# One process for both directions of a state recurrence, and a later low part of the weights

## The chip, the cores and the metric

The kernel runs on one core of a Trainium2 chip. The metric is device time in microseconds of one launch, the median over several executions. The engines are TensorE (PE in the profile; PEld is its weight load), VectorE (DVE), ScalarE (ACT), GpSimd (POOL) and SyncE (SP, here a queue for DMAs). Each works through its own queue in program order.

## The reference

It is one layer of a bidirectional encoder, applied with one set of weights to a prompt (512 tokens) and a sample (1024 tokens), width 1024, all in fp32:

```
x = x + 0.5 * gate1 * rmsnorm(swiglu_1(mod(rmsnorm(x))))
z = mod(rmsnorm(x)) @ w_in
x = x + gate2 * rmsnorm([pool_mixer(z_pool) | rwkv7(z_rwkv)] @ w_out)
x = x + 0.5 * gate3 * rmsnorm(swiglu_2(mod(rmsnorm(x))))
```

What the change touches is the recurrence inside `rwkv7`: 8 heads of 64, forward and reversed, each with a 64 x 64 state S:

```
def step(S, inp):
    r_t, w_t, k_t, v_t, na_t, b_t = inp
    sa = einsum('bhvk,bhk->bhv', S, na_t)
    S = S * w_t + sa[..., None] * b_t + v_t[..., None] * k_t
    y = einsum('bhvk,bhk->bhv', S, r_t)
```

## The kernel before, in words

**Dense work.** The tokens stand in three blocks of 512 (two of the sample, one of the prompt), features on the partitions. Every fp32 product with a big weight matrix is made of three matmuls in a reduced fp32 format: high part of the weight by high part of the data, high by low, low by high (`mm3`, line 740). `WStream` (line 483) brings the weights in tiles of 128 x 512 in the order in which they are used: a DMA on SP's queue into one of 5 raw buffers (`wraw`), a copy on ScalarE that rounds to the high part (`whi`, 5 buffers), and a subtraction for the low part (`wlo`, 5 buffers), on GpSimd or VectorE, and during the scan always on VectorE. `get` (line 510) hands out tile i and first writes into the program the high and low parts up to tile i + 3 and the loads up to tile i + 8.

**The scan.** The recurrence is done in chunks of L = 64 tokens. Four chunks make a group (256 tokens); a macro is two groups (`gi` 0 and 1) of one pair of heads, for both directions `d`. There are 12 macros, so 24 groups and 96 chunk steps, each for two directions. For each group `scan_prep` (line 1159) makes the decays and the products between the chunk's keys (ending in a masked copy to `MU`, flag `ba`). `scan_inv` (line 1284) inverts the triangular matrices, in 31 dependent steps on VectorE for gi = 0 and on GpSimd for gi = 1; only one of the two holds the lock `inv` at a time. Then `scan_state` (line 1332) goes through the chunks in three stages:

- W: `SBD` (the state of the two heads as a block diagonal) times `AR`, plus a product of `MA` with the values in `UV`, into a PSUM bank of the direction, partitions 0 to 63, and from there by ScalarE to `iw` (a part of `XN`). In the profile these are `sb<-SBD,AR` and `sb<-MU` (64*64), then ACT `XN<-sb`. Then ScalarE makes `s0p`, the state times its decay.
- U: `MA` times that, also into partitions 0 to 63 (`sb<-XN,MU`), and by ScalarE to the upper half of `UV` (ACT `MU<-sb`).
- Last stage: the update of the state (`sb<-MU,BKt`) and the output (`sb<-AR,SBD` and `sb<-MU` with 128*64), head 0 into partitions 0 to 63 and head 1 into 64 to 127; then VectorE adds to `s0p` and writes the state (`SBD<-sb,PL,s0p`).

In the first chunk of a pair of heads the state is zero, and the products with it are left out. After the last state step of a group `scan_prep` may go on to the same group of the next macro, and at the end of a pair of heads `scan_post` (line 1399) normalizes the output and stores it (`m<-yT`).

**What sets the order.** The kernel writes all instructions in one program order, worked out when it is built. The dense work and each part of the scan are processes (Python generators) with a priority. `Estimate` (line 42) keeps an estimated clock for each engine, and `run_until` (line 217) goes on with the ready process of the highest priority. A process that yields WAIT is ready again 200 ns (state steps) or 400 ns (others) after the estimated end of all that it has just issued. Before the change the two directions are two processes of `scan_state` (line 1585), each with its own readiness; dense work yields after each matmul and fills what is left. Dense work meets the scan twice: `wout_gen(0)` (line 1486) needs the sample's output of the scan, and the output projections of the other blocks need the scan's end (`wouts`, line 1532).

Of the kernel before, what the change touches and what calls it, by code (L numbers as in the profile page):

```python
# [10 lines left out]
F32R = mybir.dt.float32r  # L11
I32 = mybir.dt.int32
AF = mybir.ActivationFunctionType
ALU = mybir.AluOpType
# [3 lines left out]
P = 128  # L18
# [4 lines left out]
TB = 512  # L23
L = 64
# [14 lines left out]
GO, WAIT, CHAIN, PIPE = -1.0, -2.0, -3.0, -4.0  # L39
# [125 lines left out]
def rev(ap):  # L165
    a = [list(x) for x in ap.ap]
    st, n = a[-1]
    a[-1] = [-st, n]
    return bass.AP(tensor=ap.tensor, offset=ap.offset + st * (n - 1), ap=a)
# [3 lines left out]
def encoder_kernel(ctx, tc, x_prompt, x_sample, c_prompt, c_sample, ada_w, ada_b, n1_pre, n1_post,  # L173
# [5 lines left out]
    V, S, G, T, SY = (Queue(est, *q) for q in (("V", nc.vector), ("S", nc.scalar), ("G", nc.gpsimd), ("T", nc.tensor),  # L179
                                               ("Y", nc.sync)))  # L180
# [3 lines left out]
    def nm(s):  # L184
        uid[0] += 1
        return f"{s}{uid[0]}"
# [15 lines left out]
    def mt(shape, tag, bufs, dt=F32, pool=None):  # L202
        return est.ring((pool or mp).tile(shape, dt, name=nm(tag), tag=tag, bufs=bufs), (id(pool), tag), bufs)
# [4 lines left out]
    class Proc:  # L208
        def __init__(self, gen, prio):
            self.gen, self.prio, self.ready, self.cond = gen, prio, est.free["T"], None  # L210
# [3 lines left out]
    def spawn(gen, prio):  # L214
        procs.append(Proc(gen, prio))
# [38 lines left out]
    flags = set()  # L254
    scanning = []
# [22 lines left out]
    def has(*k):  # L278
        return lambda: all(x in flags for x in k)

    def mm(out, lhsT, rhs, start=True, stop=True):
        T.matmul(out, lhsT, rhs, start=start, stop=stop, skip_group_check=True)
# [200 lines left out]
    class WStream:  # L483
        def __init__(self, items):
            self.items, self.raw, self.out = items, {}, {}
            self.i, self.nl, self.ns = 0, 0, 0

        def load(self, upto):
            while self.nl <= min(upto, len(self.items) - 1):
# [6 lines left out]
        def split(self, upto):  # L496
            while self.ns <= min(upto, len(self.items) - 1):
                self.load(self.ns)
                t = self.raw.pop(self.ns)
                wh = mt([P, TB], "whi", 5, F32R)  # L500
                wl = mt([P, TB], "wlo", 5, F32R)
                S.activation(wh, t, AF.Copy)
                now = est.free["T"]
                g_, v_ = max(now, est.free["G"]) + 1200, max(now, est.free["V"]) + 600
                E = G if not scanning and (g_ < now + POOL_LATE or g_ < v_) else V
                E.tensor_tensor(wl, t, wh.bitcast(F32), ALU.subtract)
                self.out[self.ns] = (wh, wl)
                self.ns += 1

        def get(self):  # L510
            i = self.i
            self.i += 1
            self.split(i + 3)
            self.load(i + 8)
            return self.out.pop(i)

    def cols(w, c0):
# [434 lines left out]
    GT = (TB, 2 * TB)  # L952
# [192 lines left out]
    GL = 4 * L  # L1145

    def st_(sb, shape, tag, bufs=1):
        return mt(shape, tag, bufs, pool=sb.sp)
# [180 lines left out]
            flags.add(("inv", m, gi))  # L1329
            give("inv")  # L1330

    def scan_state(sb, d):
        AR, BKt, UV, MA, MR, SBD, PL, bank = sb.AR, sb.BKt, sb.UV, sb.MA, sb.MR, sb.SBD, sb.PL, sb.bank[d]
        Wp = bank[0:64, 0:P]
        Up = bank[0:64, P:2 * P]
        for m, (i_, hf) in enumerate(macros):
            g, p = pairs[i_]
            nblk = GT[g] // GL
            nh = nblk // 2
            for c8 in range(8):  # L1340
                gi, c = c8 // 4, c8 % 4
                if c == 0:
                    yield has(("inv", m, gi))
                zero = hf == 0 and c8 == 0
                lastc = hf == nh - 1 and c8 == 7
                us = [gi * 16 + d * 8 + h * 4 + c for h in range(2)]
                if not zero:
                    mm(Wp, AR[:, gi, d, c, 0, :], SBD[:, d, :], stop=False)
                for h in range(2):
                    mm(Wp[:, h * L:(h + 1) * L], MA[64:128, us[h], :], UV[64:128, gi, d, c, h, :], start=zero)  # L1350
                wsb = sb.iw[:, d * P:(d + 1) * P]
                S.activation(wsb, Wp, AF.Copy)
                if not zero and not lastc:
                    s0p = st_(sb, [P, P], f"s0p{d}")
                    S.activation(s0p, SBD[:, d, :], AF.Copy, scale=PL[:, m % 2, gi, d, c:c + 1])
                yield WAIT
                for h in range(2):
                    mm(Up[:, h * L:(h + 1) * L], MA[0:64, us[h], :], wsb[:, h * L:(h + 1) * L])
                S.activation(UV[0:64, gi, d, c].rearrange("p h f -> p (h f)"), Up, AF.Copy)
                yield WAIT  # L1360
                if not lastc:
                    for h in range(2):
                        hs_ = slice(64 * h, 64 * h + 64)
                        mm(bank[hs_, 0:L], BKt[:, gi, d, c, hs_], UV[:, gi, d, c, h, :])
                yo = 256 + c * L
                if not zero:
                    for h in range(2):
                        hs_ = slice(64 * h, 64 * h + 64)
                        mm(bank[hs_, yo:yo + L], SBD[hs_, d, hs_], AR[hs_, gi, d, c, 1, :], stop=False)
                for h in range(2):  # L1370
                    mm(bank[64 * h:64 * h + 64, yo:yo + L], UV[:, gi, d, c, h, :], MR[:, us[h], :], start=zero)
                if not lastc:
                    for h in range(2):
                        hs_ = slice(64 * h, 64 * h + 64)
                        pl_ = PL[hs_, m % 2, gi, d, c:c + 1]
                        if zero:
                            V.tensor_scalar(SBD[hs_, d, hs_], bank[hs_, 0:L], pl_, None, op0=ALU.mult)
                        else:
                            V.scalar_tensor_tensor(SBD[hs_, d, hs_], bank[hs_, 0:L], pl_, s0p[hs_, hs_],
                                                   ALU.mult, ALU.add)  # L1380
                if c == 3:
                    t = 2 * hf + gi
                    gb = t if d == 0 else nblk - 1 - t
                    if t == 0 and i_ not in sb.yT:
                        if i_ >= 1:
                            yield has(("post", i_ - 1))
                        if i_ not in sb.yT:
                            sb.yT[i_] = st_(sb, [P, GT[g]], "yT")
                    o = sb.yT[i_][:, gb * GL:(gb + 1) * GL]
                    if d == 1:  # L1390
                        o = rev(o)
                    if t >= nh:
                        V.tensor_tensor(o, o, bank[:, 256:512], ALU.add)
                    else:
                        S.activation(o, bank[:, 256:512], AF.Copy)
                    flags.add(("st", m, gi, d))
                yield WAIT

    def scan_post(sb):
# [181 lines left out]
    with tc.tile_pool(name="late", bufs=1, reuse_waits="tile") as lp:  # L1581
        sb = ScanBufs(lp)
        scanning.append(sb)

        spawn(scan_state(sb, 0), 0)
        spawn(scan_state(sb, 1), 0)
        spawn(scan_inv(sb, 0), PRIO_INV)
        spawn(scan_inv(sb, 1), PRIO_INV)
        spawn(scan_prep(sb), PRIO_PREP)
        spawn(scan_post(sb), PRIO_POST)  # L1590

        run_until(has(("m", 1), ("m", 0)))
        scanning.clear()
# [35 lines left out]
```

## Time and profile before

| | us |
|---|---|
| three runs | 3784.39, 3785.25, 3792.80 |
| median | 3785.25 |
| the profiled execution | 3780.28 |
| its span, first to last instruction | 3778.3 |
| TensorE busy | 3593.2 (95%) |
| VectorE busy | 1999.0 (53%) |
| ScalarE busy | 1424.1 (38%) |
| GpSimd busy | 1410.4 (37%) |

The mean granted clock of TensorE is 0.956. The first state step is at 1270.6 us of the span and the last at 2697.4 us. In a row of a group, `out<-in` names tiles, `xN` counts instructions, and behind the bars stand the busy time and the idle time in front of them with what ended it. All instructions are recorded at one helper's line (161), so tiles tell them apart. An fp32 matmul leaves two records. The window rows give busy time per engine in a stretch and the granted clock; the timeline rows give start, duration, engine, instruction; the rows of waits give who waited for whom, the total in us, how often, and the longest.

### The profile page before, as it was taken

The page shows a single profiled execution, that of the slowest core. Times are in us where ns is not written, and L with a number is a line of the kernel's source. Part 1 is how long each engine was busy: PE and PEld are TensorE (multiplying, and loading weights), DVE is VectorE, ACT ScalarE, POOL GpSimd, SP SyncE. Part 2 cuts the span into 40 slices and gives each one's busy share as a digit, 9 for nine tenths or more (in the row PEclk, how much of TensorE's full clock was granted, in tenths as well). Part 3 has the DMA queues.
Part 4 walks back from the last instruction along what each step waited for, and adds up shares of the span by engine and source line. Part 5 has one row for each costly group of instructions (what it writes and reads, how often), then busy time and mean ns, then how long its engine had stood idle before and what let it go on. Part 6 is the DMA issues. An engine that isn't in the chain of part 4 may idle for free. (4 is left out here: it accounts for less than half of the span.)

```text
span 3778.3 us, 53665 instructions
## 1 busy us (share of the span) xinstructions
PE 3593.2 (95%) x19579; PEld 2703.6 (72%) x19579; DVE 1999.0 (53%) x3801; ACT 1424.1 (38%) x2776; POOL 1410.4 (37%) x1716
## 2 busy tenths in 40 slices
PE   7999999998999999999899989799999999999998
PEld 4667878876676767666666666567787778877886
DVE  3128362237237778776777776778448622242223
ACT  3324342225335434344345433343334432234222
POOL 2333444443132222234234233432344344444444
PEclk8999999998999999999889978599999999999999
DMA  7655343334344322222324343222254333334332
GB/s 274 235 181 169 91 154 92 99 90 134 123 128 126 93 67 88 82 71 87 117 76 122 96 137 105 74 73 77 87 159 151 103 115 98 93 109 132 94 95 78
DMA packets 557980, 432.11 MB, mean 114 GB/s; under 512 B 27029, under 2 KB 511572, under 8 KB 553620
## 3 DMA queue, kind: packets, MB, share of 16 engines
q1 hardware_dynamic: 524900, 379.90, 32.8%
q10 hardware_dynamic: 32816, 48.78, 4.1%
q8 instruction: 155, 2.54, 0.3%
q14 instruction: 109, 0.89, 0.1%
HBM read 367.23 MB, written 61.34 MB: 113 GB/s over the span
## 5 line engine op out<-in xcount | busy, mean ns | idle before, releaser
L161 POOL TENSOR_TENSOR wlo<-wraw,whi 128x512 fp32r<-128x512 f32 x672 | 892.6, 1346 | 1294.2 <-ACT whi L161 866.5
L161 DVE TENSOR_TENSOR y<-y,y 128x512 f32<-128x512 f32 x480 | 327.2, 684 | 848.9 <-PE y L161 847.9
L161 ACT ACTIVATE whi<-wraw 128x512 fp32r<-128x512 f32 x938 | 559.2, 622 | 181.6 <-PE v L161 139.7
L161 PE MATMUL u<-hh,whi 128*128 128x512 f32 x1392 | 568.2, 408 | 10.2 <-ACT zraw L161 4.0
L161 PE MATMUL u<-hl,whi 128*128 128x512 f32 x1392 | 564.3, 405 | 14.1 <-POOL hl L161 7.4
L161 PE MATMUL v<-hh,whi 128*128 128x512 f32 x1392 | 562.4, 404 | 12.8 <-ACT hh L161 7.6
L161 PE MATMUL u<-hh,wlo 128*128 128x512 f32 x1392 | 567.0, 407 | 0.1
L161 PE MATMUL v<-hl,whi 128*128 128x512 f32 x1392 | 561.0, 403 | 1.0 <-DVE hl L161 1.0
L161 PE MATMUL v<-hh,wlo 128*128 128x512 f32 x1392 | 560.7, 403 | 0.0
L161 PE MATMUL y<-gh,whi 128*128 128x512 f32 x1056 | 425.6, 403 | 12.8 <-DVE y L161 10.8
L161 PE MATMUL y<-gl,whi 128*128 128x512 f32 x1056 | 422.7, 400 | 0.2 <-DVE gl L161 0.2
L161 PE MATMUL y<-gh,wlo 128*128 128x512 f32 x1056 | 422.2, 400 | 0.0
L161 POOL TENSOR_TENSOR XN<-XN 64x126 f32<-64x126 f32 (+22 forms) x744 | 322.4, 433 | 93.6 <-DVE XN L161 18.5
L161 PEld LDWEIGHTS u<-hl,whi 128*128 128x128 f32 x1392 | 266.6, 191 | 81.5 <-DVE hl L161 12.6
L161 ACT ACTIVATE gh<-s 128x512 fp32r<-128x512 f32 x132 | 83.3, 631 | 639.3 <-DVE s L161 639.3
L161 PEld LDWEIGHTS u<-hh,whi 128*128 128x128 f32 x1392 | 266.3, 191 | 80.9 <-issue 7.7
L161 PEld LDWEIGHTS v<-hh,whi 128*128 128x128 f32 x1392 | 264.2, 190 | 82.9 <-ACT hh L161 11.3
L161 PEld LDWEIGHTS u<-hh,wlo 128*128 128x128 f32 x1392 | 266.3, 191 | 68.8 <-issue 9.5
L161 PEld LDWEIGHTS v<-hl,whi 128*128 128x128 f32 x1392 | 264.4, 190 | 66.3 <-issue 4.9
L161 PEld LDWEIGHTS v<-hh,wlo 128*128 128x128 f32 x1392 | 264.8, 190 | 62.9 <-issue 5.9
L161 DVE TENSOR_TENSOR wlo<-wraw,whi 128x512 fp32r<-128x512 f32 x266 | 206.4, 781 | 150.6 <-ACT whi L161 149.8
L161 PEld LDWEIGHTS y<-gh,whi 128*128 128x128 f32 x1056 | 199.9, 189 | 67.2 <-DVE y L161 12.0
(252 smaller groups left out, 4504.6 us busy)
## 6 DMA issues: line engine op xcount, KB each, us to landing
wraw<-in_f_w_dram SPq DMA_DIRECT2D x792, 256.0 KB
ada<-in_ada_w_dram SPq DMA_DIRECT2D x32, 1024.0 KB
wraw<-in_w_in_dram SPq DMA_DIRECT2D x98, 256.0 KB
xk<-xs ACTq DMA_DIRECT2D x96, 256.0 KB
xs<-y ACTq DMA_DIRECT2D x48, 256.0 KB
wraw<-in_w_out_dram SPq DMA_DIRECT2D x48, 256.0 KB
in_k<-zk SPq DMA_DIRECT2D x48, 128.0 KB
in_kk<-zkk SPq DMA_DIRECT2D x48, 128.0 KB
```

What stands on the lines that cost most here:

```text
L161: return f(*args, **kw)
```

## The change

`scan_state` becomes one process for both directions. The second direction's W and U now go to partitions 64 to 127 of its own bank, the matmuls of the two directions take turns, and ScalarE copies them back to partitions 0 to 63 of `iw` and `UV`. The copies to `s0p` move from the W stage to behind U's copies. In the last stage the four state matmuls stand together, then the outputs of direction 0 and of direction 1. `WStream` makes high parts up to tile i + 3 as before, but during the scan low parts only up to tile i + 2 and loads up to tile i + 7; outside it nothing changes.

```
     def split(self, upto):
         while self.ns <= min(upto, len(self.items) - 1):
             self.load(self.ns)
-            t = self.raw.pop(self.ns)
-            wh = mt([P, TB], "whi", 5, F32R)
+            self.high(self.ns)
+            t, wh = self.raw.pop(self.ns), self.hi.pop(self.ns)
             wl = mt([P, TB], "wlo", 5, F32R)
-            S.activation(wh, t, AF.Copy)
...
+    def high(self, upto):
+
+        while self.nh <= min(upto, len(self.items) - 1):
+            self.load(self.nh)
+            wh = mt([P, TB], "whi", 5, F32R)
+            S.activation(wh, self.raw[self.nh], AF.Copy)
+            self.hi[self.nh] = wh
+            self.nh += 1
+
     def get(self):
         i = self.i
         self.i += 1
-        self.split(i + 3)
-        self.load(i + 8)
+        lag = 1 if scanning else 0
+        self.high(i + 3)
+        self.split(i + 3 - lag)
+        self.load(i + 8 - lag)
         return self.out.pop(i)
...
-    def scan_state(sb, d):
-        AR, BKt, UV, MA, MR, SBD, PL, bank = sb.AR, sb.BKt, sb.UV, sb.MA, sb.MR, sb.SBD, sb.PL, sb.bank[d]
-        Wp = bank[0:64, 0:P]
-        Up = bank[0:64, P:2 * P]
+    def scan_state(sb):
+        AR, BKt, UV, MA, MR, SBD, PL = sb.AR, sb.BKt, sb.UV, sb.MA, sb.MR, sb.SBD, sb.PL
+        both = range(2)
+        half = [slice(64 * h, 64 * h + 64) for h in both]
+        Wp = [sb.bank[d][half[d], 0:P] for d in both]
+        Up = [sb.bank[d][half[d], P:2 * P] for d in both]
...
-                us = [gi * 16 + d * 8 + h * 4 + c for h in range(2)]
+                us = lambda d, h: gi * 16 + d * 8 + h * 4 + c
+                wsb = [sb.iw[:, d * P:(d + 1) * P] for d in both]
+                s0p = {}
                 if not zero:
-                    mm(Wp, AR[:, gi, d, c, 0, :], SBD[:, d, :], stop=False)
-                for h in range(2):
-                    mm(Wp[:, h * L:(h + 1) * L], MA[64:128, us[h], :], UV[64:128, gi, d, c, h, :], start=zero)
-                wsb = sb.iw[:, d * P:(d + 1) * P]
-                S.activation(wsb, Wp, AF.Copy)
+                    for d in both:
+                        mm(Wp[d], AR[:, gi, d, c, 0, :], SBD[:, d, :], stop=False)
+                for h in both:
+                    for d in both:
+                        mm(Wp[d][:, hl_(h)], MA[64:128, us(d, h), :], UV[64:128, gi, d, c, h, :], start=zero)
+                for d in both:
+                    S.activation(wsb[d], Wp[d], AF.Copy)
+                yield WAIT
+                for h in both:
+                    for d in both:
+                        mm(Up[d][:, hl_(h)], MA[0:64, us(d, h), :], wsb[d][:, hl_(h)])
+                for d in both:
+                    S.activation(UV[0:64, gi, d, c].rearrange("p h f -> p (h f)"), Up[d], AF.Copy)
                 if not zero and not lastc:
-                    s0p = st_(sb, [P, P], f"s0p{d}")
-                    S.activation(s0p, SBD[:, d, :], AF.Copy, scale=PL[:, m % 2, gi, d, c:c + 1])
-                yield WAIT
-                for h in range(2):
-                    mm(Up[:, h * L:(h + 1) * L], MA[0:64, us[h], :], wsb[:, h * L:(h + 1) * L])
-                S.activation(UV[0:64, gi, d, c].rearrange("p h f -> p (h f)"), Up, AF.Copy)
+                    for d in both:
+                        s0p[d] = st_(sb, [P, P], f"s0p{d}")
+                        S.activation(s0p[d], SBD[:, d, :], AF.Copy, scale=PL[:, m % 2, gi, d, c:c + 1])
                 yield WAIT
                 if not lastc:
-                    for h in range(2):
-                        hs_ = slice(64 * h, 64 * h + 64)
-                        mm(bank[hs_, 0:L], BKt[:, gi, d, c, hs_], UV[:, gi, d, c, h, :])
+                    for d in both:
+                        for h in both:
+                            mm(sb.bank[d][half[h], 0:L], BKt[:, gi, d, c, half[h]], UV[:, gi, d, c, h, :])
+                yo = slice(256 + c * L, 256 + c * L + L)
+                for d in both:
+                    if not zero:
+                        for h in both:
+                            mm(sb.bank[d][half[h], yo], SBD[half[h], d, half[h]], AR[half[h], gi, d, c, 1, :], stop=False)
+                    for h in both:
+                        mm(sb.bank[d][half[h], yo], UV[:, gi, d, c, h, :], MR[:, us(d, h), :], start=zero)
...
-        spawn(scan_state(sb, 0), 0)
-        spawn(scan_state(sb, 1), 0)
+        spawn(scan_state(sb), 0)
```

What follows in the step (the state's sums on VectorE, and the output's copy at the group's end) is the same, written for both directions one after the other.

More of the change, by code (lines that the diff above doesn't have):

```diff
@@ L485, in __init__ @@
             self.items, self.raw, self.out = items, {}, {}
-            self.i, self.nl, self.ns = 0, 0, 0
+            self.i, self.nl, self.ns, self.nh, self.hi = 0, 0, 0, 0, {}
         def load(self, upto):
@@ L1330, in scan_inv @@
             give("inv")
-    def scan_state(sb, d):
-        AR, BKt, UV, MA, MR, SBD, PL, bank = sb.AR, sb.BKt, sb.UV, sb.MA, sb.MR, sb.SBD, sb.PL, sb.bank[d]
-        Wp = bank[0:64, 0:P]
-        Up = bank[0:64, P:2 * P]
+    def scan_state(sb):
[4 more added lines that the diff above has]
+        Up = [sb.bank[d][half[d], P:2 * P] for d in both]
+        hl_ = lambda h: slice(h * L, (h + 1) * L)
         for m, (i_, hf) in enumerate(macros):
@@ L1360, in scan_state @@
+                if not zero and not lastc:
+                    for d in both:
+                        s0p[d] = st_(sb, [P, P], f"s0p{d}")
+                        S.activation(s0p[d], SBD[:, d, :], AF.Copy, scale=PL[:, m % 2, gi, d, c:c + 1])
                 yield WAIT
                 if not lastc:
-                    for h in range(2):
-                        hs_ = slice(64 * h, 64 * h + 64)
-                        mm(bank[hs_, 0:L], BKt[:, gi, d, c, hs_], UV[:, gi, d, c, h, :])
-                yo = 256 + c * L
@@ L1366, in scan_state @@
[L1366 to L1371, printed above, removed]
-                if not lastc:
[L1373 to L1380, printed above, removed]
+                    for d in both:
+                        for h in both:
+                            mm(sb.bank[d][half[h], 0:L], BKt[:, gi, d, c, half[h]], UV[:, gi, d, c, h, :])
@@ new lines, in scan_state @@
+                yo = slice(256 + c * L, 256 + c * L + L)
[5 more added lines that the diff above has]
+                        mm(sb.bank[d][half[h], yo], UV[:, gi, d, c, h, :], MR[:, us(d, h), :], start=zero)
+                if not lastc:
+                    for d in both:
+                        for h in both:
+                            pl_ = PL[half[h], m % 2, gi, d, c:c + 1]
+                            if zero:
+                                V.tensor_scalar(SBD[half[h], d, half[h]], sb.bank[d][half[h], 0:L], pl_, None, op0=ALU.mult)
+                            else:
+                                V.scalar_tensor_tensor(SBD[half[h], d, half[h]], sb.bank[d][half[h], 0:L], pl_,
+                                                       s0p[d][half[h], half[h]], ALU.mult, ALU.add)
@@ L1381, in scan_state @@
                 if c == 3:
                     t = 2 * hf + gi
-                    gb = t if d == 0 else nblk - 1 - t
-                    if t == 0 and i_ not in sb.yT:
+                    if t == 0:
                         if i_ >= 1:
                             yield has(("post", i_ - 1))
[L1387 to L1396, printed above, removed]
+                        sb.yT[i_] = st_(sb, [P, GT[g]], "yT")
+                    for d in both:
+                        gb = t if d == 0 else nblk - 1 - t
+                        o = sb.yT[i_][:, gb * GL:(gb + 1) * GL]
+                        if d == 1:
+                            o = rev(o)
+                        if t >= nh:
+                            V.tensor_tensor(o, o, sb.bank[d][:, 256:512], ALU.add)
+                        else:
+                            S.activation(o, sb.bank[d][:, 256:512], AF.Copy)
+                        flags.add(("st", m, gi, d))
```

## The prediction

> **What bounds the kernel now.** I read the page first, then the busy time of each engine in stretches of 50 us, then the timeline of TensorE inside the scan, then the list of who waited for whom there. The change touches the scan alone (state steps, and the weight stream while the scan runs), so only the stretch from 1200 to 2715 us matters. Its sum, and four of the 29 stretches from 1250 to 2700 (columns: window, length, then busy us and instructions of PE, PEld, DVE, ACT, POOL, then TensorE's granted clock, DMA share, GB/s):
>
> ```profile
> 1200.00:2715.00 1515.00, 1428.75 (x10072) 1014.97 (x10071) 1107.14 (x2477) 630.51 (x1428) 488.81 (x933) 0.92 0.30 90
> ```
> ```profile
> 1250.00:1300.00 50.00, 48.89 (x374) 35.32 (x373) 34.12 (x67) 20.40 (x48) 23.81 (x55) 1.00 0.24 69
> ...
> 2250.00:2300.00 50.00, 48.05 (x291) 32.68 (x291) 28.88 (x47) 18.42 (x48) 33.44 (x69) 0.61 0.32 103
> ...
> 2400.00:2450.00 50.00, 43.21 (x237) 27.42 (x236) 33.10 (x55) 23.99 (x50) 32.70 (x65) 0.57 0.13 39
> ...
> 2650.00:2700.00 50.00, 49.10 (x402) 34.02 (x402) 19.77 (x42) 15.02 (x42) 10.25 (x28) 1.00 0.17 54
> ```
>
> The reader is to see two kinds of stretch. In 21 of the 29 (the first and the last quoted are of them) TensorE is busy 44 us of 50 or more at a clock of 0.90 to 1.00: it sets the pace. In the other eight (2250 and 2400 are examples) the clock has fallen: dense work waits for a normalization or for the scan. VectorE, the next, is busy 1107 of 1515 us, 73%. So time taken off TensorE comes out of the end in 21/29 = 72% of the scan, and little of it elsewhere.
>
> What a state step costs TensorE now (start, duration, instruction; each fp32 matmul leaves two records, and I go from start to start, since ends are modelled):
>
> ```profile
> 2006.55 0.43 PE L161 MATMUL sb<-SBD,AR 128*64 128x128 f32 x2
> 2006.91 0.44 PE L161 MATMUL sb<-MU 64*64 64x64 f32 x4
> 2007.28 0.43 PE L161 MATMUL sb<-SBD,AR 128*64 128x128 f32 x2
> ...
> 2008.02 0.50 PE L161 MATMUL v<-hh,whi 128*128 128x512 f32 x1
> ...
> 2008.91 0.44 PE L161 MATMUL sb<-XN,MU 64*64 64x64 f32 x4
> 2009.28 0.70 PE L161 MATMUL sM<-in_wa,w2s 64*128 64x256 f32 x4
> ...
> 2010.28 0.50 PE L161 MATMUL v<-hh,whi 128*128 128x512 f32 x1
> 2010.62 0.40 PE L161 MATMUL v<-hl,whi 128*128 128x512 f32 x1
> 2010.94 0.34 PE L161 MATMUL sb<-MU,BKt 128*64 128x64 f32 x4
> 2011.21 0.33 PE L161 MATMUL sb<-AR,SBD 64*64 64x64 f32 x4
> 2011.47 0.34 PE L161 MATMUL sb<-MU 128*64 128x64 f32 x4
> 2011.74 0.50 PE L161 MATMUL v<-hh,wlo 128*128 128x512 f32 x1
> ```
>
> The W stage of one direction is 2006.55 to 2007.28: 0.36 us for the product with the state and 0.37 us for the pair with UV. U is 0.37 us (2008.91 to 2009.28). The state update with both output products is 0.80 us (2010.94 to 2011.74). One direction costs 1.90 us, both 3.80 us a step. In W and U all results of both directions go to partitions 0 to 63. In the last stage the two heads already go to partitions 0 to 63 and 64 to 127, and there a pair takes 0.26 us instead of 0.37.
>
> **The change part by part.** *W and U in alternating halves.* The second direction now writes partitions 64 to 127, and the matmuls alternate. What an alternating pair costs when it isn't followed by another array shape is seen in a first step of a scan, where the products with the zero state are missing:
>
> ```profile
> 2000.83 0.34 PE L161 MATMUL sb<-MU,BKt 128*64 128x64 f32 x4
> 2001.00 0.29 PE L161 MATMUL sb<-MU 128*64 128x64 f32 x4
> 2001.11 0.29 PE L161 MATMUL sb<-MU,BKt 128*64 128x64 f32 x4
> 2001.23 0.29 PE L161 MATMUL sb<-MU 128*64 128x64 f32 x4
> ```
>
> Pairs that alternate start 0.11 to 0.12 us after one another: two matmuls in the time that two records of one column half need (of the 0.37 us pair, about 0.11 for the first load, twice 0.06, and the rest the change to the next shape). So I take both directions together at what one costs now: W 0.73 instead of 1.47 (2006.55 to 2008.02), U 0.37 instead of 0.74. Saved: 0.74 + 0.37 = 1.11 us a step. The other bound: no overlap, only a longer run in one shape. Here both U stages happen to stand together:
>
> ```profile
> 1500.55 0.68 PE L161 MATMUL sb<-XN,MU 64*64 64x64 f32 x8
> 1501.15 0.50 PE L161 MATMUL u<-hl,whi 128*128 128x512 f32 x1
> ```
>
> That is 0.60 us for both, saving 0.14 and not 0.37. I take the overlap, since the pairs above that alternate have the same rows of the array and differ in columns alone, as the new ones do; they are 128 rows high and the new ones of UV and U are 64, so the other end stays in the range.
>
> [...]
>
> *Last stage in one process.* Four state matmuls stand in one shape: 0.27 + 0.11 = 0.38 us; then for each direction 0.26 + 0.27 as now: 1.44 us instead of 1.59, or less of a gain where both directions stand together already. I take 0.10 us.
>
> *Fewer visits.* A dense matmul in its stream starts 0.23 us after the last; beside a visit it takes 0.34 (2010.28 to 2010.62) and 0.32 (2010.62 to 2010.94), so a visit costs 0.20 us besides its own matmuls.
>
> ```profile
> 2003.33 0.39 PE L161 MATMUL v<-hh,wlo 128*128 128x512 f32 x1
> 2003.56 0.39 PE L161 MATMUL v<-hh,whi 128*128 128x512 f32 x1
> ```
> ```profile
> 1270.59 0.68 PE L161 MATMUL sb<-MU 64*64 64x64 f32 x8
> ...
> 2697.44 0.34 PE L161 MATMUL sb<-MU 128*64 128x64 f32 x4
> ```
>
> From the first of these two rows to the last, the timeline of TensorE has 368 runs of such instructions between others, 3.83 for each of 96 steps; with one process it is 3. Saved: 0.83 x 0.20 = 0.17 us.
>
> Sum: 1.11 + 0.10 + 0.17 = 1.38 us in each of the 88 steps with a state, 121 us, and about 0.9 us (0.37 for W, 0.37 for U, 0.17) in the eight without, 7 us: 128 us of TensorE. Times 72%: **-92 us**; bounds: none of it on the path (0), all of it (-128).
>
> *Low parts one tile later.* VectorE makes all low parts during the scan, and now stops for the high part:
>
> ```profile
> DVE wlo L161 <- ACT whi L161: 127.7, 75, 5.5
> ```
>
> The 127.7 us (75 stops, 5.5 at the longest) go. In the stretches that TensorE paces they cost nothing, since VectorE then waits for the next result of TensorE instead. In the other 28% it is up to 36 us, and I take **-10 us**. Behind such a stop stand the next VectorE work (inverse steps, state sums, masks) and, on SP's queue, the weight load that wants the freed raw tile; it is issued behind the same low part as before, for a tile one nearer. What it can cost:
>
> ```profile
> L161 DVE TENSOR_TENSOR wlo<-wraw,whi x245: 635/685/1777, 1202.9 to 2711.6; 128x512 fp32r<-128x512 f32 x123
> ```
>
> A scan of 1515 us uses 245 tiles, 6.2 us each, so a low part still has two tiles, 12 us, of lead against a longest stop of 5.5 us, which itself goes. I take 0; without that cover a matmul would wait in dense runs, some 2 us in one tile in ten, 50 us.
>
> *Both directions in lockstep.* Each stage waits for the later direction, and the scaled state copies now stand behind U's copies:
>
> ```profile
> L161 ACT ACTIVATE s0p<-SBD,PL 128x128 f32<-128x128 f32 x160 | 62.5, 391 | 0.2
> ...
> L161 ACT ACTIVATE XN<-sb 64x128 f32<-64x128 f32 x192 | 50.7, 268 | 195.7 <-PE sb L161 159.1 <-DVE XN L161 11.7 <-issue 11.1
> ```
>
> Two scaled copies (the first row) are 0.78 us, less than the 1.44 us of matmuls that follow, so on the chip they are covered by these; in the planner's order of the program they move the last stage back. At worst a step is longer by the other direction's W pair and U (0.37 + 0.37) its two copies (0.27 each, the second row) and the 0.78: 2.06 us. Where TensorE paces, other work fills it. In the other 28%, 27 steps, it is 0 to 56 us, and I take a quarter, **+14 us**, as each stage is also shorter.
>
> The sum is -92 - 10 + 14 = -88 us. The profiled execution took 3780.28 us (span 3778.3), 5 us below the median of 3785.25: 3780.3 - 88 = 3692, and on the scale of the medians 3697.
>
> **The rivals.** *No overlap in 64 rows* (the change doesn't do what it says). W and U gain only what a longer run gives: 0.14 for W's pairs, 0.15 for its products with the state (the part of 0.36 that I put to the change of shape, as in a pair), 0.14 for U, with 0.10 + 0.17 as above 0.70 us a step, 66 us in all, 47 on the path, with -10 and +14 a sum of -43: 3742. For it: no 64-row pair with equal rows and different columns is in the trace. Against: the 128-row pairs. [...] Chance 0.13.
>
> *The scan's own chain paces.* The inverse of one group waits for that of the other, 24 in a row, on VectorE and GpSimd, and TensorE's freed time then only makes dense work wait longer for the scan's output. Here is its slack (mask of the next group, and the last copy of the inverse before it):
>
> ```profile
> 1495.05 1.28 DVE L161 TENSOR_TENSOR MU<-sM,mask 128x512 f32<-128x512 f32 x2
> ```
> ```profile
> 1497.23 0.59 ACT L161 ACTIVATE MU<-sM 32x512 f32<-32x512 f32 x1 [1.85 <-PE sM L161]
> ```
> ```profile
> 1540.91 1.29 DVE L161 TENSOR_TENSOR MU<-sM,mask 128x512 f32<-128x512 f32 x2 [0.20 <-PE sM L161]
> ```
> ```profile
> 1550.05 0.59 ACT L161 ACTIVATE MU<-sM 32x512 f32<-32x512 f32 x1 [0.92 <-PE sM L161]
> ```
>
> The masks are done 1.5 and 8.4 us before the inverse lets go, so the inverse is the longer side. The first output projection starts with these loads:
>
> ```profile
> 2255.48 2.36 SPq L161 DMA_DIRECT2D y<-wp  x5
> ```
>
> Then all gains before it are lost, and those of 2450 to 2700 stay: 250 us at 14.9 us a step (1427 us for 96) are 17 steps, 23 us, with 10 for the stops: 3752. Against it: the inverse ends with TensorE work (the waits for PE sM in these rows), which comes sooner with less before it. Chance 0.14.
>
> *Slower: lockstep makes the group the longer side.* Place: from a group's last state step to its next mask. The slack is 5 us in the mean. With 2.06 us more in each of four steps a group is 8.2 us longer, 3.2 beyond the slack, 78 us over 24 groups. Dense work runs ahead meanwhile, until it needs the scan's output:
>
> ```profile
> 2712.83 0.89 SPq L161 DMA_DIRECT2D m<-yT  x2
> ```
> ```profile
> 2781.11 3.91 SPq L161 DMA_DIRECT2D y<-wp  x8
> ```
>
> These 68 us, of which I allow half for loading that output, hide 34 of the 78: +44, 3829. It decides from about 1.6 us more a step. For it: the small slack. Against: the stages are shorter on TensorE. Chance 0.11.
>
> **How the numbers follow.** The forecast has 0.62, the rivals 0.13, 0.14 and 0.11. A measurement can tell about 0.2%, 7.6 us. The forecast's own range goes from 3646 (-128 and -10) to 3748 (-92 and +56); with the first two rivals inside, 3645 to 3765 leaves out the slower one and the tails. Faster: 0.60 + 0.12 + 0.12 = 0.84; same: 0.06, slower: 0.10.
>
> **What would show it.** Right: W rows of both directions start within 0.01 us of one another and a step's W takes about 0.73 us, U 0.37; 288 visits or nearly; the wait of wlo for whi falls from 127.7 us to under 20; TensorE's time on state work falls by about a third; the scan ends 60 us sooner or more. Wrong: U of both at 0.60 us (first rival); a lower clock in more stretches with a scan as long as now (second); masks that end behind the inverse's last copy and a longer scan (third); PE waiting for wlo (the lead was too short).

## The result, and the profile after

| | before | after |
|---|---|---|
| median of four runs each, us | 3784.82 | 3729.04 |
| lowest to highest | 3781.49 to 3792.80 | 3719.62 to 3732.30 |
| the profiled execution | 3780.28 | 3731.42 |
| its span | 3778.3 | 3729.7 |
| its mean granted clock | 0.956 | 0.948 |

The ratio is 0.9847, 95% interval 0.9831 to 0.9863: 58 us of 3786 faster, where 88 were forecast. The same windows as before, of the kernel after (columns: window, length, busy us and instructions of PE, PEld, DVE, ACT, POOL, granted clock, DMA share, GB/s), and one more, 1450 to 1500:

```profile
1250.00:1300.00 50.00, 45.41 (x361) 32.76 (x359) 34.19 (x58) 22.11 (x50) 29.28 (x66) 1.00 0.27 81
1450.00:1500.00 50.00, 47.14 (x307) 33.88 (x307) 37.40 (x83) 18.47 (x41) 13.79 (x26) 0.76 0.28 85
2250.00:2300.00 50.00, 48.42 (x373) 34.97 (x371) 39.94 (x86) 20.90 (x49) 20.17 (x38) 0.93 0.38 111
2400.00:2450.00 50.00, 48.55 (x385) 35.01 (x383) 42.74 (x103) 24.28 (x54) 7.99 (x16) 1.00 0.30 88
2650.00:2700.00 50.00, 49.41 (x274) 39.02 (x275) 25.25 (x47) 17.02 (x35) 14.97 (x10) 1.00 0.42 132
1200.00:2715.00 1515.00, 1395.59 (x10292) 1008.11 (x10291) 1141.88 (x2517) 667.10 (x1463) 504.00 (x935) 0.90 0.31 95
```

In the sum TensorE has 33 us less busy time than before in the same stretch (1428.75 there) and a lower clock (0.92 there), and VectorE 35 us more busy time (1107.14 there). The two stretches of a low clock that were quoted of before, 2250 and 2400, are dense now, but others have lost their clock, such as 1450. Of the 29 stretches of 50 us from 1250 to 2700 nine are granted less than 0.90 (seven before).

A state step in the timeline of TensorE after (start, duration, instruction):

```profile
2537.14 0.44 PE L161 MATMUL sb<-SBD,AR 128*64 128x128 f32 x4
2537.51 0.45 PE L161 MATMUL sb<-MU 64*64 64x64 f32 x8
2537.89 0.50 PE L161 MATMUL v<-hh,whi 128*128 128x512 f32 x1
...
2539.01 0.45 PE L161 MATMUL sb<-XN,MU 64*64 64x64 f32 x8
2539.39 0.50 PE L161 MATMUL v<-hl,whi 128*128 128x512 f32 x1
...
2541.44 0.45 PE L161 MATMUL sb<-MU,BKt 128*64 128x64 f32 x8
2541.82 0.33 PE L161 MATMUL sb<-AR,SBD 64*64 64x64 f32 x4
2542.08 0.34 PE L161 MATMUL sb<-MU 128*64 128x64 f32 x4
2542.34 0.33 PE L161 MATMUL sb<-AR,SBD 64*64 64x64 f32 x4
2542.61 0.34 PE L161 MATMUL sb<-MU 128*64 128x64 f32 x4
2542.87 0.50 PE L161 MATMUL y<-gh,whi 128*128 128x512 f32 x1
```

Both directions now stand in one row each of W's two products: 0.37 and 0.38 us, 0.75 together. U takes 0.38 (2539.01 to 2539.39) and the last stage 1.43 (2541.44 to 2542.87). Over the scan the timeline has 285 visits of state matmuls where there were 368, and from start to start they take 282 us where they took 377. (A row that stands ahead of a wait is counted as 2 us at most, here and below; with the waits taken out altogether it is 265 where it was 365.)

The waits of VectorE from 1200 to 2715, after (total us, times, longest):

```profile
DVE y L161 <- PE y L161: 90.9, 40, 5.7
...
DVE wlo L161 <- ACT whi L161: 10.2, 5, 6.0
```

The stops of low parts went from 127.7 to 10.2 us. The end of the scan and the first load of the last output projection on SP's queue (start, duration):

```profile
2677.91 0.82 SPq L161 DMA_DIRECT2D m<-yT  x2
...
2729.12 3.87 SPq L161 DMA_DIRECT2D y<-wp  x8
```

The first came 35 us sooner than before, the second 52.

### The profile page after: what moved, and what is told of

Its sections match the earlier page's. It is cut to its first block, busy times and chain, and to the rows that moved or that the text cites. A ratio compares the mean times of both kernels' runs of the same rounds, so it can differ in the third digit from the quotient of the medians.

```text
span 3729.7 us, 53665 instructions
## 1 busy us (share of the span) xinstructions
PE 3511.1 (94%) x19579; PEld 2656.5 (71%) x19579; DVE 2014.5 (54%) x3817; ACT 1443.7 (39%) x2778; POOL 1399.6 (38%) x1700
## 5 line engine op out<-in xcount | busy, mean ns | idle before, releaser
L161 POOL TENSOR_TENSOR XN<-XN 64x126 f32<-64x126 f32 (+22 forms) x744 | 331.2, 445 | 177.3 <-DVE XN L161 60.7
L161 PEld LDWEIGHTS u<-hh,wlo 128*128 128x128 f32 x1392 | 268.4, 193 | 70.2 <-issue 10.2
L161 PEld LDWEIGHTS y<-gh,wlo 128*128 128x128 f32 x1056 | 200.8, 190 | 51.3 <-DVE wlo L161 3.7
```

Source lines behind the costliest of these rows:

```text
L161: return f(*args, **kw)
```

## The experiments

Twelve kernels, each timed in rounds beside the kernel before on the same chip. "us" in the text is the ratio times 3786 (about the median of before in these rounds), less 3786, so that kernels of different chips can be set side by side; an interval of a ratio is about 6 us to each side, so a difference of two kernels is known to some 8 us. The clock is the mean over all runs of the kernel.

| kernel | ratio to before (95%) | us | clock |
|---|---|---|---|
| before | 1 | 0 | 0.953 |
| after | 0.9847 (0.9831 to 0.9863) | -58 | 0.949 |
| e1: before with late low parts | 0.9995 (0.9981 to 1.0008) | -2 | 0.954 |
| e2: after without late low parts | 0.9931 (0.9919 to 0.9943) | -26 | 0.941 |
| e3: after, W and U in one half | 0.9889 (0.9877 to 0.9902) | -42 | 0.953 |
| e4: after, scaled state in stage W | 0.9854 (0.9841 to 0.9867) | -55 | 0.949 |
| e5: after, one half, no late low parts | 0.9961 (0.9948 to 0.9974) | -15 | 0.948 |
| e6: after with more matmuls | 1.0026 (1.0016 to 1.0036) | +10 | 0.958 |
| e7: before with more matmuls | 1.0302 (1.0288 to 1.0316) | +114 | 0.953 |
| e8: after without the lock of the inverse | 0.9836 (0.9817 to 0.9855) | -62 | 0.948 |
| e9: after without low parts in the scan | 0.9662 (0.9647 to 0.9677) | -128 | 0.959 |
| e10: before without low parts in the scan | 0.9863 (0.9842 to 0.9883) | -52 | 0.960 |
| e11: after, other costs in the planner | 0.9940 (0.9926 to 0.9954) | -23 | 0.947 |
| e12: e2's order, low parts late | 0.9882 (0.9862 to 0.9901) | -45 | 0.942 |

The theory after the result: the overlap is there as forecast, but time freed on TensorE is worth much less than 72%, since VectorE and the waits for it stand close beside it. Its rivals: the overlap is not there and the gain is that of the low parts; the chain of inverses paces; the lockstep gives back what the overlap gains. Where a text on record gives a theory a letter, the letter stands for what that text, or an earlier one, says beside it; what follows from each run is told in words.

**The late low parts alone (e1).** The kernel before, with the new `WStream`:

```
-            self.split(i + 3)
-            self.load(i + 8)
+            lag = 1 if scanning else 0
+            self.high(i + 3)
+            self.split(i + 3 - lag)
+            self.load(i + 8 - lag)
```

> The kernel before with the later low parts alone. Theory A (TensorE's freed time is the gain, and the scan's own chain keeps part of it): the stops of VectorE for the high part go from 127.7 us to under 15, and the time falls by 5 to 15 us, to about 3775. Theory B (the gain is the stops of VectorE): most of the 56 us is here, 3745 or less. Theory C (the alternating halves bring 90 us and the lockstep takes 35 back): about 3775.

It gained nothing that can be measured (-2 us). The waits of VectorE from 1200 to 2715, first of before, then of e1:

```profile
DVE y L161 <- PE y L161: 38.1, 19, 4.3
...
DVE SBD L161 <- issue: 18.6, 6, 4.8
```
```profile
DVE y L161 <- PE y L161: 78.8, 36, 6.4
DVE SBD L161 <- PE sb L161: 60.1, 38, 8.3
DVE SBD L161 <- issue: 48.0, 15, 5.6
...
DVE wlo L161 <- ACT whi L161: 4.5, 6, 1.3
```

The 127.7 us of stops are down to 4.5, but 41 us more are waited for TensorE's `y` (78.8 against 38.1) and 29 more ahead of the state's sums (48.0 against 18.6). With two processes VectorE stops elsewhere instead. The scan by itself did become shorter: its last `m<-yT` starts at 2652.92 us in e1 and at 2712.83 in before, and the kernel is no faster for these 60 us.

**The merged process without them (e2).** After with one line changed:

```
-            lag = 1 if scanning else 0
+            lag = 0
```

> The changed kernel with low parts at their old place, so one process in alternating halves alone. A: about 3740, 10 us over the changed kernel. B: 3770 or more. C: about 3740.

-26 us, between the two times expected. So the late low parts, worth nothing in the kernel before, are worth 32 us in the merged one (-26 to -58).

**Both directions in one column half (e3).** After, with the second direction's W and U in partitions 0 to 63 again; the order of all queues is that of after:

```
-        Wp = [sb.bank[d][half[d], 0:P] for d in both]
-        Up = [sb.bank[d][half[d], P:2 * P] for d in both]
+        Wp = [sb.bank[d][half[0], 0:P] for d in both]
+        Up = [sb.bank[d][half[0], P:2 * P] for d in both]
```

> The changed kernel, but W and U of both directions go to partitions 0 to 63, so that nothing overlaps there; the order of the program is the same in every queue. U of both should take 0.60 us and W about 1.15 instead of 0.38 and 0.75, some 60 us of TensorE in all. A: about 60 percent of this reaches the end, 3765. B: 3735. C: all of it does, 3785 or more, which is as slow as before.

The timeline of TensorE in e3, W and U of one step:

```profile
2542.49 0.65 PE L161 MATMUL sb<-SBD,AR 128*64 128x128 f32 x4
2543.07 0.68 PE L161 MATMUL sb<-MU 64*64 64x64 f32 x8
2543.68 0.50 PE L161 MATMUL v<-hh,whi 128*128 128x512 f32 x1
...
2544.80 0.68 PE L161 MATMUL sb<-XN,MU 64*64 64x64 f32 x8
2545.40 0.50 PE L161 MATMUL v<-hl,whi 128*128 128x512 f32 x1
```

In one half W's products take 0.58 and 0.61 us and U 0.60, in alternating halves 0.37, 0.38 and 0.38. The single records in the trace agree: in this U the matmuls of the two directions start 7 ns after one another in after (2539.121 and 2539.128) and 58 ns in e3 (2544.906 and 2544.964), as in before where both stand together (1500.657 and 1500.715). So the overlap is real, also for 64 rows, and that rival falls. It frees 54 us on TensorE (335.3 us of state work in e3, 281.6 in after), and it is worth 16 us: 30%, where 60 percent, none or all of it had been expected. The whole windows from 1200 to 2700, first of e3, then of after, show where the rest is:

```profile
1200.00:2700.00 1500.00, 1403.51 (x10199) 1032.95 (x10198) 1136.38 (x2508) 633.83 (x1450) 492.70 (x928) 0.92 0.31 94
```
```profile
1200.00:2700.00 1500.00, 1380.59 (x10227) 995.84 (x10226) 1134.83 (x2509) 660.31 (x1451) 494.91 (x929) 0.90 0.31 95
```

TensorE is idle for 23 us more. And its clock is lower: counted as one less the clock, times the time, 176 us are lost in e3's runs in the mean and 191 in after's, 15 more. 16 + 23 + 15 is the 54 that were freed. That it comes out so evenly is chance, as the idle time is of one profiled execution and the rest of all runs: between the two profiled executions alone 8 us reach the end, 23 are idle and 31 go with the clock.

For what TensorE waits there, from 1200 to 2700, first e3, then after:

```profile
PE sM L161 <- DVE MU L161: 26.4, 24, 4.1
...
PE sb L161 <- DVE SBD L161: 12.9, 21, 1.8
```
```profile
PE sM L161 <- DVE MU L161: 35.8, 23, 4.1
PE sb L161 <- DVE SBD L161: 17.0, 26, 2.2
```

All rows of these lists together, the waits for VectorE come to 76 us in e3 and 96 in after, all others to 19 and 23. So nearly all of the added idle time is spent waiting for VectorE, which is busy for the same time in both, 1136 and 1135 us, 76%.

**One half and no late low parts (e5).** Both edits, of e2 and e3, together.

> One process for both directions, W and U in one column half, low parts at their old place: neither the overlap nor the later low parts. Theory D (the later low parts pay only where TensorE has slack, and the overlap only where VectorE doesn't stop): 3760 to 3770, so that the overlap without the later low parts is worth under 10 us. Theory A (each part pays by itself, 15 us for the overlap, 31 for the low parts): 3775.

-15 us, what theory A had. All queues have e2's order. With e2, e3 and after this makes a square: the overlap is worth 11 us without the late low parts (e5 to e2, where state work falls from 358 to 309 us from start to start, 49 freed) and 16 with them, the late low parts 27 in one half (e5 to e3) and 32 with the overlap. Within their errors the two add; what the low parts need is the merged process, not the overlap. The merging itself, without either, gains 15 us together with the order that it brings.

The windows of e5 and of e2 show again where the rest of the overlap went:

```profile
1200.00:2700.00 1500.00, 1382.83 (x10054) 1014.89 (x10052) 1105.47 (x2475) 615.43 (x1423) 472.55 (x917) 0.90 0.30 91
```
```profile
1200.00:2700.00 1500.00, 1364.05 (x10118) 982.56 (x10118) 1113.69 (x2499) 644.11 (x1433) 474.12 (x918) 0.88 0.30 91
```

In e2 TensorE is idle for 19 us more, and 25 us more of its clock are lost (223 in place of 198, means of five runs each). Here the waits for VectorE grow by 7 us only (68 to 75) and those for ScalarE by 12 (39 to 51), so VectorE isn't the only one that TensorE then waits for.

**The scaled state back in stage W (e4).** The block that makes `s0p` stands ahead of the first `yield WAIT` again, for both directions, and no longer behind U's copies:

```
                     S.activation(wsb[d], Wp[d], AF.Copy)
+                if not zero and not lastc:
+                    for d in both:
+                        s0p[d] = st_(sb, [P, P], f"s0p{d}")
...
                 yield WAIT
```

> The changed kernel with the scaled copies of the state back in the W stage, so that in the planner's order the last stage no longer waits for them. A: within 10 us of the changed kernel, 3720 to 3740. C: most of what the lockstep takes comes back, 3700 to 3715. B: no change.

-55 us against -58 of after, inside the intervals: where `s0p` is made makes no difference that can be measured, the planner's order moving a little with it.

**More matmuls (e6, e7).** In after each step repeats U's four matmuls six times, in before each direction's two matmuls three times, unknown to the planner, so that the rest keeps its order; e6's edit:

```
+                for _ in range(6):
+                    for h in both:
+                        for d in both:
+                            nc.tensor.matmul(Up[d][:, hl_(h)], MA[0:64, us(d, h), :], wsb[d][:, hl_(h)],
+                                             start=True, stop=True, skip_group_check=True)
```

> The changed kernel with its eight records of U repeated six times in each step, which the planner doesn't see, so that the order of all else stays: about 1.38 us of TensorE more in each of 96 steps, 132 us. Theory D (TensorE has slack now and its freed time was filled by waits and a lower clock): under half of it reaches the end, 3730 + 40 to 65 = 3770 to 3795. Theory A (TensorE still sets the pace in 72 percent): + 95, 3825.

> The kernel before with the U pair of each direction repeated three times, unseen by the planner: 0.70 us for each of 192, 133 us in all. The step of the prediction, 72 percent on the path: + 96, about 3882. If TensorE has slack here too: + 60 or less, 3845.

The added rows of e6 and of e7 (records; least, median and longest in ns; first and last start):

```profile
L1379 PE MATMUL sb<-XN,MU x4608: 218/218/311, 1261.6 to 2726.3; 64*64 64x64 f32 x192
```
```profile
L1359 PE MATMUL sb<-XN,MU x2304: 218/218/366, 1275.5 to 2814.3; 64*64 64x64 f32 x192
```

From start to start U's rows go from 50 to 192 us in e6 and from 80 to 230 in e7, so 142 and 150 us are added. They cost 68 and 114 us: 48% on top of after, 76% on top of before, so the 72% of the prediction holds there and no longer holds in after. In e6 the rest comes back from what after had lost. The window of e6, like those of e3 and after above:

```profile
1200.00:2700.00 1500.00, 1424.32 (x14318) 1068.18 (x14318) 1108.30 (x2454) 639.68 (x1403) 472.05 (x919) 0.92 0.30 90
```

TensorE is busy for 44 us more than in after (1424.32 against 1380.59), and of the clock 161 us are lost in place of 191; 68 + 44 + 30 is 142. TensorE's waits for VectorE are down from 96 us to 57. In e7 the clock stays at that of before.

**No lock of the inverse (e8).** After without the two lines that keep the inverses of the two groups apart:

```
-            yield from take("inv")
...
-            give("inv")
```

> The changed kernel without the lock between the two inverses, so that the one on VectorE and the one on GpSimd may run at once. If the chain of inverses paces the scan now: the scan ends at least 20 us sooner and the time falls to 3710 or less. If VectorE's load or the state group paces it: within 10 us of 3729.

The end of the scan on SP's queue, e8:

```profile
2630.54 0.81 SPq L161 DMA_DIRECT2D m<-yT  x2
```

The scan ends 47 us sooner than in after (2677.91), and the time is the same (-62 against -58, intervals overlap). So the chain of inverses doesn't pace this kernel in the way that the rival has it. (The planner's order changed with the lock, and by e11 below an order alone can move the time by 35 us, so a smaller worth of that chain isn't excluded.) Like e1, it also shows that the end of the scan isn't what sets the end of the kernel.

**No low parts of weights in the scan (e9, e10).** In after and in before VectorE's subtraction is left out during the scan, and the third matmul uses the high part in its place:

```
+                if scanning:
+                    self.out[self.ns] = (wh, wh)
+                    self.ns += 1
+                    continue
                 wl = mt([P, TB], "wlo", 5, F32R)
```

> The changed kernel without the low parts of the weights during the scan: the third matmul takes the high part again, so TensorE does as much and VectorE about 185 us less (the low product of that stretch is left out of the result). Theory F (the waits that ate the freed TensorE time come from VectorE's load): TensorE's idle time in the scan falls from 119 us to under 80, and the time by 40 us or more, to 3690 or less. Theory G (they come from the order and from the latency of short chains, whatever VectorE's load): within 15 us of 3729.

> The kernel before without the low parts during the scan, as in the run beside it (the low product of that stretch is left out of the result). F: TensorE sets the pace there, so 185 us less of VectorE gives only 10 to 25 us, about 3770. G: the same as in the changed kernel, whatever that is.

The groups of instructions from 1200 to 2715, of before and of after (busy us and mean ns behind the first bar), show what is left out:

```profile
L161 DVE TENSOR_TENSOR wlo<-wraw,whi 128x512 fp32r<-128x512 f32 x245 | 186.1, 765 | 128.4 <-ACT whi L161 127.7
```
```profile
L161 DVE TENSOR_TENSOR wlo<-wraw,whi 128x512 fp32r<-128x512 f32 x253 | 191.8, 764 | 10.8 <-ACT whi L161 10.2
```

Some 186 us of VectorE gave 52 us in before and 192 us gave 70 in after: 28% and 36%. (The planner knows of what is left out, so the order is another one too, and the two shares are rough.) In before 10 to 25 us were expected, as TensorE was thought to set the pace nearly alone; that falls too. VectorE's time was worth something before the change, and is perhaps worth somewhat more after it. In both, the clock rises to 0.96 (150 us lost in e9 and 148 in e10), though TensorE's work is the same, and TensorE waits less for VectorE, 60 us in e9 where it was 96, 39 in e10 where it was 54. From 1200 to 2715 e9 is idle for 84 us on TensorE where after was for 119, a little over the 80 that theory F had.

**Other costs in the planner (e11).** After, with the estimate of TensorE's durations set nearer to the new rows: a dense matmul 231 ns and not 218, W's product with the state 185 ns and not 269, a state matmul of 64 columns 110 ns and not 125 (64 rows) or 78 (128 rows):

```
-                cost = n / 2.35
+                cost = n / 2.22
...
+            elif m == 64 and n == 128 and k == 128:
+                cost = 185.0
+            elif m == 64 and n == 64:
+                cost = 110.0
```

> The changed kernel with the planner's costs of matmuls nearer to the rows of its trace: dense 512/2.22 = 231 ns instead of 218, a matmul of 64 columns of weights by 64 about 110 ns and the 128 by 64 by 128 one 185 ns. G: an order that fits the chip takes waits away, 3700 to 3720. F: no more than 10 us.

-23 us: 35 us of after's gain are gone, where some gain was expected. The work is the same but for 17 of VectorE's 3817 instructions, which the planner now gives to GpSimd; what differs is the order in which it is issued, and it does so from the kernel's beginning, not in the scan alone.

**Late low parts in an unchanged order (e12).** The planner reckons with e2's places, so that every queue keeps e2's order, but each low part and the load behind it are issued one tile later. From the edit, against e2:

```
+                est.op(E.key, "tensor_tensor", (s, t, wh.bitcast(F32)), {})
...
-            lag = 0
+            lag = 1 if scanning else 0
             self.high(i + 3)
+            self.plan_load(i + 8)
+            self.low(i + 3 - lag)
```

> The kernel with one process alone (e2, 3761 us), and low parts one tile later while the planner still reckons with their old place: each queue has the same instructions in the same places as there, only that each low part (and the load behind it) is that of the tile before. Theory S (the stops of VectorE are what the later low parts save): the stops go from 103 us to about 10 and the time to about 3730, like the changed kernel. Theory O (what pays is the other order that the planner comes to): 3750 to 3761, though the stops go.

The waits of VectorE from 1200 to 2700, e2, then e12:

```profile
DVE wlo L161 <- ACT whi L161: 103.3, 72, 8.5
```
```profile
DVE wlo L527 <- ACT whi L161: 12.7, 6, 4.6
```

91 us of stops go, and 19 us are gained (-26 to -45), which lies between the two theories. The other 13 us of the late low parts' 32 (to -58) come with the order that the planner makes when it knows of them; known to some 9 us, they are little more than the error.

## Why the prediction was right and wrong

The sign and the range held; the gain was 58 us and not 88. That the sum came this near is in part luck, since two errors went against one another: the overlap, the merging and the lockstep gave 52 us less than forecast (-26 and not -78), and the late low parts 22 us more (-32 and not -10). By the steps:

**The overlap in W and U: right in its mechanism.** A step takes 0.75 and 0.38 us there, 0.73 and 0.37 were forecast. e3 and after read the same partitions and differ only in the half that the second direction's W and U are written to: a pair of stages takes 0.60 us in one half and 0.38 in two, and in two halves the weight loads of the two directions start 6 ns after one another (2539.068 and 2539.074 in the U above).

**The size of it: 112 us of TensorE, 128 forecast.** State rows lost 95 us (377 to 282) and 83 visits at 0.20 us are 17. One part that was missing: the two W stages don't always stand together, since the second direction's state sums come later. The timeline of TensorE, after, with the wait and what ended it in brackets:

```profile
1550.16 0.43 PE L161 MATMUL sb<-SBD,AR 128*64 128x128 f32 x2 [0.85 <-DVE SBD L161]
1550.80 0.43 PE L161 MATMUL sb<-SBD,AR 128*64 128x128 f32 x2 [0.20 <-DVE SBD L161]
```

In 12 of the 88 steps the row of W's product is split in two like this. Matmuls at half clock, longer ones, are in the 282 us too: U of both takes 0.62 us at 1487.53 of after, where the granted clock is 0.50, and 0.38 at 1498.14, where it is 1.00.

**"Times 72%": the step that failed.** It took the share of stretches in which TensorE is busy nearly throughout for the worth of each microsecond taken off it. For time added to before that was right: 76% (e7). For the time that the change takes off it was not: in the merged kernel the overlap alone was worth 22 to 30% (11 us of 49, 16 of 54), and at after's level even added time costs only 48%. (Time taken off in before's own order wasn't measured.) The rest went to waits, 19 and 23 us, and to a lower clock, 25 and 15 us in the means of the runs. VectorE, at 73% in the mean, was named as the next and then not reckoned with. In the same 1515 us it now has 35 us more to do, and 186 us taken off it in before were already worth 52 (e10). That two engines which wait for one another share the path, so that the worth of each falls as it is relieved, fits these numbers; it isn't shown by itself, since no run relieved VectorE and changed TensorE's work in one order. What remained of the forecast's merging, overlap and lockstep, -78, was -26 (e2).

**The late low parts: -10 forecast, -2 alone, -32 in the merged process.** The reason given, that VectorE then waits for TensorE's next result, is what e1 shows. That it is worth more once TensorE's state work is merged wasn't foreseen; e12 gives 19 us to the stops themselves. Beside it, "I take 0" for the cover was nearly right: TensorE now waits for a late low part twice, and its own list of waits, after, says

```profile
PE y L161 <- DVE wlo L161: 2.5, 2, 2.2
```

where before had no such wait. The last section shows what one of them led to.

**Lockstep: +14 forecast, none seen.** Merging without the overlap or the late low parts gained 15 us (e5), and the place of `s0p` costs nothing that can be measured (e4). A cost that the new order outweighs isn't excluded. The slower rival falls with the result itself.

**The rivals.** Without the overlap a sum of -43 was worked out; e3 measured -42. That is chance: its late low parts were worth 27 and not 10, its merging 15 and not 33. The chain of inverses doesn't pace (e8).

**The signs.** The W rows, the visits and the stops came as listed. State work fell by a quarter, not a third; the scan ended 35 us sooner, not 60, and e8 shows that this sign told little of the kernel's time.

**Open.** e11 moved the time by 35 us by the order alone. So the 15 us of merging and the 13 us that e12 leaves aren't settled in their cause: each goes with another order, and a merged kernel in the order of before wasn't tried.

## What to carry to other kernels

The share of the time in which an engine is busy throughout priced the work that was added to it here (72% forecast, 76% measured), and not the work that was taken off. Before pricing the latter, look at the next engine: beside one that was three quarters busy, 22 to 30% came out. An experiment that repeats existing work, or leaves some out, without changing the order gives this exchange rate directly. Where an order is planned from estimates, compare edits in the same order, since another order alone can move the time by a good part of the edit (35 us beside 58 here).

## What the hardware showed that was not expected

**A wait of two microseconds was followed by 23 at half clock in one kernel, and hardly any in another.** e3 and after have the same order, and at the same place of the one execution that was profiled of each, TensorE waits for a late low part, 2.13 us in e3 and 2.16 in after. The timeline of TensorE there, e3, then after:

```profile
1480.36 0.50 PE L161 MATMUL y<-gh,wlo 128*128 128x512 f32 x1 [2.13 <-DVE wlo L161]
```
```profile
1473.86 0.80 PE L161 MATMUL y<-gh,wlo 128*128 128x512 f32 x1 [2.16 <-DVE wlo L161]
```

The 9 us up to shortly before the wait's end and the 23 us behind them, as windows of e3 and of after (the granted clock is the third number from the end):

```profile
1471.00:1480.00 9.00, 7.23 (x44) 5.43 (x43) 7.71 (x23) 2.25 (x5) 0.00 (x0) 1.00 0.39 112
1480.00:1503.00 23.00, 22.54 (x196) 16.23 (x197) 16.51 (x26) 11.38 (x28) 13.60 (x26) 0.93 0.23 70
```
```profile
1464.50:1473.50 9.00, 7.20 (x44) 5.41 (x42) 7.71 (x23) 2.26 (x5) 0.00 (x0) 1.00 0.38 112
1473.50:1496.50 23.00, 22.64 (x145) 15.47 (x146) 15.39 (x23) 10.40 (x23) 9.81 (x20) 0.50 0.19 59
```

Ahead of the wait both run at full clock. Behind it e3 falls to half clock for a moment (0.93 in the mean), and after stays at half for the whole 23 us, though TensorE is busy in both for more than 22: it gets through 145 records in place of 196. In the traces of before and after each stretch of one clock, but for the last of the trace, is a whole multiple of 3.41 us long (43 stretches and 75). Here e3 is at half clock for one such stretch (from 1481.66), after for seven, 23.89 us (from 1473.64). The stretch of 3.41 us just ahead of the fall, e3, then after:

```profile
1478.25:1481.66 3.41, 1.20 (x23) 0.89 (x24) 2.71 (x6) 2.19 (x4) 0.00 (x0) 1.00 0.04 12
```
```profile
1470.23:1473.64 3.41, 1.47 (x7) 0.89 (x5) 2.71 (x5) 1.80 (x4) 0.00 (x0) 1.00 0.03 7
```

In both TensorE is busy for less than half of it, 1.20 and 1.47 us. So the half clock came behind stretches with 2.21 and 1.94 idle us of 3.41, and in after TensorE was busy for 23.68 us of the 23.89 that it lasted. What makes the difference in the time that it lasts isn't settled.

**Less work on TensorE came with a lower clock.** With the overlap the mean clock went from 0.953 (e3, its runs from 0.950 to 0.956) to 0.949 (after, 0.947 to 0.951) and from 0.948 (e5) to 0.941 (e2), with 142 us of matmuls added to after up to 0.958 (e6), with VectorE relieved to 0.959 (e9). What sets the clock isn't shown by these runs. In the means of the runs some 15 of the overlap's 54 us went there (e3 to after) and 25 of its 49 (e5 to e2).
